# Attention: a unit's inverted sums are turned by their transfer to DRAM, not on TensorE, and the order is planned anew

## The chip, the cores and the metric

The kernel runs on one core of one Trainium2 chip. The metric is the device time of one execution in microseconds; lower is better. The engines are TensorE (PE, with its weight loads shown as PEld), VectorE (DVE), ScalarE (ACT), GpSimd (POOL) and SyncE (SP). SP computes nothing: it issues most transfers, one after the other, and waits in order for what each needs. The transfers themselves run on 16 DMA engines.

## The reference

One layer of a diffusion transformer over 1,024 latent tokens (width 1,024) with 256 context tokens, all in float32. Both attention branches have 8 query heads of width 64 in 2 groups of 4, one key and value head for each group:

- branch 0 (A): keys within 128 tokens of the query, and all 256 context keys; a "sink" logit for each head joins the softmax's sum;
- branch 1 (B): all 1,024 + 256 keys, queries and keys normalised (RMS).

```python
def _sink_softmax(scores, sink):
    sink = sink.astype(jnp.float32)[:, :, None, None]
    m = jnp.maximum(jnp.max(scores, axis=-1, keepdims=True), sink)
    e = jnp.exp(scores - m)
    return e / (jnp.sum(e, axis=-1, keepdims=True) + jnp.exp(sink - m))

def _global_attention(q, k_all, v_all):       # blocks of 128 queries
    ...
        p = jax.nn.softmax(_gqa_scores(q_blk, k_all), axis=-1)
        return _gqa_values(p, v_all)
```

Both branches' outputs go through a matrix each, are weighted by sigmoid gates, merged and projected; then come a residual with layer norm, a feed-forward block with a convolution of width 3 over the tokens, and another layer norm. The change touches only the division by the softmax's sum.

## The kernel before

The kernel has three stages: the projections (to about 325 us of the profiled execution), attention with the branch matrices of branch 0 and part of branch 1 (to about 732 us), and the merge, the projection, the feed-forward block and the norms (to the end).

**Units.** Attention is cut into 32 units, `Unit(br, i, g)`: units 0 to 15 are branch 0, units 16 to 31 branch 1; `i` is the block of 128 queries, `g` the group of four heads. A unit does this:

- POOL splits its queries into a high part that TensorE's fast float32 form keeps and the rest (`qhi`, `qlo`). PE turns them (`qtr`), ACT copies them (`qcp`), and two SP transfers make a second copy with the halves of its partitions swapped (`qdm`, lines 747 and 748, "the `q` swap"). Only then can the unit's scores be computed.
- For each head PE computes scores (`sc`, lines 759 and 760), DVE takes them out of PSUM with their maximum (`pm`), and ACT takes the exponential with its sum (`ex`). The sums of the four heads are the columns of a tile `sm`, 128 partitions (queries) by 4.
- DVE inverts them (`norm`, lines 819 to 821, planned as `nr`).
- PE turns the exponentials block by block (`tr`, line 847) into the `pt` buffers of PSUM. ACT or POOL makes a high part and DVE or POOL the rest, and PE multiplies both with the values (`av`, line 856). This output has the head's width on its partitions and the four heads' queries along its rows.
- ACT copies it out (`avs`), POOL adds its halves (`up`, `ot`, line 861), multiplies them with the inverted sums (`tt`, line 1259), and splits the product for the branch matrix (`oh`, `ol`).

**The inverted sums on their way.** The multiplication `tt` needs them along the row, the same in every partition of a head, while `sm` has the queries on partitions. Before the change, four steps do this:

1. `st` (line 824): PE turns `sm` into 4 rows of 128 in a `pt` buffer of PSUM.
2. `rc` (line 829): ACT copies these into the first partitions of `rb`.
3. `dn` (line 833): SP writes them to a DRAM tile of 4 x 128.
4. `rb` (line 837): after `dn` has landed, SP reads them back twice, each time to 64 partitions with the same two rows in all of them.

```python
def turn(self, tr):
    nc.tensor.transpose(tr[0:4, 0:P], self.sm, ident)
    self.str = tr

def row(self, rb):
    self.rb = rb
    nc.scalar.copy(rb[0:4, 0], self.str[0:4, 0:P])

def rowout(self):
    self.dn = dpool.tile([4, P], F32, tag=f"dn{self.id}", name=f"dn{self.id}")
    nc.sync.dma_start(self.dn, self.rb[0:4, 0])
```

**What sets the order.** In the attention stage no engine's order follows the text. `graph` makes all steps with their dependences, buffers and keys (`KEY`, in units of a unit's number: `st` of unit 3 in branch 0 has the key 3 + 1.27). `plan` then goes through time: on each engine it takes, among the next `LOOK` = 24 steps in the order of keys that could start, the one with the smallest key within `SLACK` of the earliest start. How long a step holds its engine and when its result is there comes from `COST`, for example `dn=(SP, .30, 2.2)`: it holds SP for 0.30 us and has landed 2.2 us after its start. The steps are then issued in the order of their planned starts, and each engine runs them in that order, whatever the true durations are. `FILL` places the groups of the branch matrix among the units of branch 1. Rings of buffers limit how far engines run ahead: 3 `pt` buffers, 2 of `s`, 1 of `av`, 2 of `rb`, 2 each of `q1` and `q2` (the queries and their swapped copy).

Of the kernel before, what the change touches and what calls it, by code (L numbers as in the profile page):

```python
# [13 lines left out]
P = 128  # L14
# [25 lines left out]
PWB = 5  # L40
DAH = 3
SINK = 640
POOLED, FILL, SUMS = ((0,), (1, 6)), (16.988136, 27.931), ('ot1', 'ot1')
LOOK, SLACK = 24, (0, 0, 0, 0, 0)
D3AT = (7, 5), (7, 9), (4, 1), (4, 4), (4, 7), (4, 10), (5, 2)
NXS = 5
RAWB = 3
# [18 lines left out]
PE, ACT, DVE, POOL, SP = range(5)  # L66
# [19 lines left out]
def plan(ops, rings, free, look, slack):  # L86
    todo = [sorted((o for o in ops if o.eng == e), key=lambda o: o.key) for e in range(5)]
    for o in ops:
        for b in o.uses:
            b.left += 1  # L90
    port, done = 0.0, []
    while any(todo):
        best = None
        for e in range(5):
            ready = []
            for o in todo[e][:look]:
                if any(d.end is None for d in o.after):
                    continue
                r = max([free[e]] + [d.end for d in o.after] + [b.free(rings) for b in o.takes])
                if o.port:  # L100
                    r = max(r, port)
                if r < BIG:
                    ready.append((r, o))
            if ready:
                least = min(r for r, _ in ready) + slack[e]
                pick = min((c for c in ready if c[0] <= least), key=lambda c: c[1].key)
                if best is None or pick[0] < best[0]:
                    best = pick
        r, o = best
        todo[o.eng].remove(o)  # L110
        o.start, o.end = r, r + o.lat
        free[o.eng] = r + o.occ
        if o.port:
            port = r + o.occ
        for b in o.takes:
            b.slot = rings[b.ring].index(b.free(rings)) if b.fix is None else b.fix
            rings[b.ring][b.slot] = BIG
        for b in o.uses:
            b.left -= 1
            b.end = max(b.end, o.end)  # L120
            if b.left == 0:
                rings[b.ring][b.slot] = b.end
        done.append(o)
    return sorted(done, key=lambda o: o.start)
# [4 lines left out]
    sc0=(PE, .70, .945), sc1=(PE, .91, 1.16), scx=(PE, .94, 1.19),  # L129
    pm0=(DVE, .80, .97), pm1=(DVE, 1.26, 1.43), pmx=(DVE, .40, .56),  # L130
    ex0=(ACT, .83, .98), ex1=(ACT, 1.14, 1.30), exx=(ACT, .49, .65),
    nr0=(DVE, .18, .28), nr1=(DVE, .34, .44), st=(PE, .11, .36), rc=(ACT, .20, .34), dn=(SP, .30, 2.2),
    rb=(SP, 1.25, 3.1),
    tr=(PE, .436, .685), hi=(ACT, .47, .675), lo=(DVE, .605, .765), cp=(ACT, .47, .675), ph=(POOL, .59, .70),
    pl=(POOL, 1.27, 1.38), avh=(PE, .233, .485), avl=(PE, .233, .485),
# [8 lines left out]
PRING = "pt", "s", "av"  # L144
RINGS = dict(pt=3, s=2, av=1, qs=1, q1=2, q2=2, p=8, hi=4, lo=4, ptr=2, up=1, ot=1, rb=2, wraw=1, wh=1, wl=1)

KEY = {'qh': -0.919337, 'qt': -1.197497, 'sc': -0.139853, 'scs': (0.199825, 0.270357),
           'scx': -3.142963, 'tr': 0.868828, 'tru': (0.216182, 0.070723),
           'av': 1.348883, 'st': 1.265771, 'out': 0.885708, 'exd': 1.273589, 'st1': 1.664154, 'wb': (27.969376, 29.459582),
           'wg': (31.81419, 33.291489, 33.170198, 33.528645), 'ge': -0.046198, 'gr': 4.26668}  # L150
UNITS = 32


def graph(x, key=KEY, pooled=((3,), (2, 6)), fill=None, ot=("ot0", "ot1")):
    ops, last = [], {}
    def op(kind, k, fn, after=(), takes=(), uses=()):
        e, occ, lat = COST[kind]
        o = Op(e, kind, occ, lat, k, fn, after, takes, uses, kind in PORT)
        ops.append(o)
        return o  # L160
# [10 lines left out]
    for hf in (0, 1):  # L171
        b = Buf("pt", 2) if hf == 0 else Buf("av", 0)
# [5 lines left out]
        for c in range(4):  # L178
            r = op("gr", key["gr"] + .6 * (4 * hf + c), lambda hf=hf, c=c: x.gr(hf, c), [e], uses=[tile])
        op("gd", key["gr"] + .6 * (4 * hf + c), lambda hf=hf: x.gd(hf), [r], uses=[tile])  # L180
    units = []
    for u in range(UNITS):
# [10 lines left out]
        if u >= 2:  # L193
            qs, pt = Buf("qs"), Buf("pt")
# [11 lines left out]
        p = {}  # L206
        nar = br == 0 and w == 256
        other = []
        if br:
            s, pc = Buf("s"), Buf("p")  # L210
# [8 lines left out]
        for h in range(4):  # L219
            k = U + key["sc"] + key["scs"][br] * h  # L220
            s = Buf("pt" if nar and h < 2 else "s")
# [27 lines left out]
                sums.append(e)  # L249
        kn = U + (key["st"], key["st1"])[br]  # L250
        n_ = op(f"nr{br}", kn - .05, lambda u=u: x.norm(u), sums)
        pt, rb = Buf("pt"), Buf("rb")
        t = op("st", kn, lambda u=u, p=pt: x.st(u, p), [n_], [pt])
        r = op("rc", kn, lambda u=u, p=pt, b=rb: x.rc(u, p, b), [t], [rb], [pt])
        dn = op("dn", kn, lambda u=u: x.dn(u), [r], uses=[rb])
        rbd = op("rb", kn, lambda u=u: x.rb(u), [dn], uses=[rb])
        rbd.lat = 6.0 if 17 <= u < 30 else 4.2
        av = Buf("av")
        avo, trs = [], []
        for j, n in enumerate(kt):  # L260
            k = U + key["tr"] + j * key["tru"][br]
            ka = U + key["av"] + j * key["tru"][br]
            pt, hi, lo = Buf("pt"), Buf("hi"), Buf("lo")
# [31 lines left out]
        f = op("ol", ko, lambda u=u: x.ol(u), [e], uses=[o_])  # L295
# [5 lines left out]
    for f2 in range(4):  # L301
# [5 lines left out]
        for f in (2 * f2, 2 * f2 + 1):  # L307
            for hf in (0, 1):
                k = f0 + (f1 - f0) * n / 16
                n += 1  # L310
                pt = Buf("pt")
# [10 lines left out]
    for f2 in (0, 1):  # L322
# [5 lines left out]
        for n in (2 * f2, 2 * f2 + 1):  # L328
            pt = Buf("pt")
# [19 lines left out]
def rings():  # L349
    return {n: [0.0] * c for n, c in RINGS.items()}  # L350
# [3 lines left out]
def layer_kernel(  # L354
# [6 lines left out]
    nc = tc.nc  # L361
# [20 lines left out]
    def ctile(shape, dt, name):  # L382
        return const.tile(shape, dt, tag=name, name=name)

    ident = ctile([P, P], F32, "ident")
# [35 lines left out]
    def ht(name, shape=(P, T), dt=F32):  # L421
        hslot[name] = pool, tag = hfree.pop(0)
        return pool.tile(list(shape), dt, tag=tag, name=name, bufs=1)
# [38 lines left out]
    sc, scc = ht("sc"), ht("scc")  # L462

    def spread(dst, src, n):
        row = ht(f"row{n}")
        hput(f"row{n}")
        nc.scalar.dma_start(row, src.partition_broadcast(P))
        nc.scalar.activation(dst, row, AF.Silu)
# [6 lines left out]
    def mod(w, row, bias, o):  # L475
        nc.vector.tensor_tensor_reduce(out=w, in0=w, in1=row, scale=1.0, scalar=bias, op0=ALU.mult, op1=ALU.add,
                                       accum_out=o)
# [6 lines left out]
    st1 = {}  # L484
# [38 lines left out]
    for n in (0, 1):  # L523
        s = slice(n * HALF, (n + 1) * HALF)
# [11 lines left out]
    for k in range(KT):  # L536
# [5 lines left out]
        for t in range(NT):  # L542
            s = slice(t * P, (t + 1) * P)
# [167 lines left out]
    class Unit:  # L711
# [108 lines left out]
                nc.vector.tensor_tensor(out=self.sm, in0=self.sm, in1=self.smc, op=ALU.add)  # L820
            nc.vector.reciprocal(self.sm, self.sm)

        def turn(self, tr):
            nc.tensor.transpose(tr[0:4, 0:P], self.sm, ident)
            self.str = tr

        def row(self, rb):
            self.rb = rb
            nc.scalar.copy(rb[0:4, 0], self.str[0:4, 0:P])  # L829

        def rowout(self):
            self.dn = dpool.tile([4, P], F32, tag=f"dn{self.id}", name=f"dn{self.id}")
            nc.sync.dma_start(self.dn, self.rb[0:4, 0])

        def rowin(self):
            for a in range(2):
                nc.sync.dma_start(self.rb[a * HD:(a + 1) * HD],
                                  self.dn.rearrange("(b a) q -> a b q", a=2)[a].partition_broadcast(HD))
# [49 lines left out]
    units = [Unit(br, i, g) for br in (0, 1) for i in range(NT) for g in range(2)]  # L888
# [80 lines left out]
    turn = [0]  # L969
# [21 lines left out]
    def at(n, fn, *only):  # L991
        if n < len(steps) and (not only or steps[n][0] in only):
            gi, k, a = steps[n]
            fn(*((gi, k) if only else (gi, k, a)))
# [13 lines left out]
    for n, (gi, k, a) in enumerate(steps):  # L1008
# [21 lines left out]
        for t in tiles:  # L1030
            if t < NT:
                s = slice(t * P, (t + 1) * P)
                x = hT[k][0][:, s], hT[k][1][:, s]
            else:
                s = slice((t - NT) * P, (t - NT + 1) * P)
                x = c[0][:, s], c[1][:, s]
# [46 lines left out]
    def small(name):  # L1083
# [3 lines left out]
                 rb=[P, 2, P], wraw=[P, 8, P], wh=[P, 8, P], wl=[P, 8, P])  # L1087
# [42 lines left out]
    class Issue:  # L1130
# [67 lines left out]
        def norm(self, u):  # L1198
            units[u].norm()

        def st(self, u, p):
            units[u].turn(at(p, f"s{units[u].id}"))

        def rc(self, u, p, b):
            units[u].row(at(b, units[u].id))

        def dn(self, u):
            units[u].rowout()

        def rb(self, u):  # L1210
            units[u].rowin()

        def tr(self, u, n, p):
            units[u].ptr(n, at(p, f"{units[u].id}_{n}"))
# [86 lines left out]
    rwb = {}  # L1301
    for o in plan(graph(Issue(), KEY, POOLED, FILL, SUMS)[0], rings(), [0.0, 2.2, 0.0, 0.0, 0.0], LOOK, SLACK):
        if o.fn:
            o.fn()
# [83 lines left out]
    wb = {2: [wq.tile([P, 8, P], R32, tag="w", name=f"{a}wb2", bufs=4) for a in "hl"]}  # L1388
# [661 lines left out]
    s = LN2_S[-1]  # L2050
# [22 lines left out]
    r = LN2_S[1]  # L2073
# [10 lines left out]
    u, ot = [], []  # L2084
# [20 lines left out]
    for t in range(nt):  # L2105
        q = slice(s.start - HALF + t * P, s.start - HALF + (t + 1) * P)
        y = sml(f"yt{t}")
        for k in range(NH):
            h, l = d3[k]
# [122 lines left out]
```

## Time and profile before

| | us |
|---|---|
| median of 3 runs | 1521.83 |
| lowest, highest | 1521.33, 1522.35 |
| the profiled execution | 1522.45 |
| its span, from first to last instruction | 1520.6 |
| mean granted TensorE clock | 0.998 of full |

Busy time in the span: PE 1507.5 us (99%), PEld 1267.1 (83%), DVE 1154.0 (76%), ACT 800.3 (53%), POOL 784.7 (52%).

How to read the rows: a row of a timeline has the start in us from the span's beginning, the duration in us, the engine, the line of the kernel, the operation and its tiles (written<-read). A row of a tile's or line's view has the durations of its instructions in ns (least/median/most) and the first and last start. "PEld" is a weight load, which overlaps the matmul before it. "SPq" is SP's own queue: its duration is that of issuing, not that of the data's way. A matmul's shown duration reaches from its entry into the array to its end, and the next one enters before that, so that work on PE is counted from start to start. In a row of waits, the number after the colon is the time in all, then how many waits, then the longest.

### The profile page before, as it was taken

The page shows a single profiled execution, that of the slowest core. Times are in us where ns is not written, and L with a number is a line of the kernel's source. Part 1 is how long each engine was busy: PE and PEld are TensorE (multiplying, and loading weights), DVE is VectorE, ACT ScalarE, POOL GpSimd, SP SyncE. Part 2 cuts the span into 40 slices and gives each one's busy share as a digit, 9 for nine tenths or more (in the row PEclk, how much of TensorE's full clock was granted, in tenths as well). Part 3 has the DMA queues.
Part 4 walks back from the last instruction along what each step waited for, and adds up shares of the span by engine and source line. Part 5 has one row for each costly group of instructions (what it writes and reads, how often), then busy time and mean ns, then how long its engine had stood idle before and what let it go on. Part 6 is the DMA issues. An engine that isn't in the chain of part 4 may idle for free.

```text
span 1520.6 us, 21967 instructions
## 1 busy us (share of the span) xinstructions
PE 1507.5 (99%) x7640; PEld 1267.1 (83%) x7640; DVE 1154.0 (76%) x1735; ACT 800.3 (53%) x1406; POOL 784.7 (52%) x743
## 2 busy tenths in 40 slices
PE   9999999999999999999999999999999999999997
PEld 7888888889988888888888998888888888888886
DVE  7588847629777777787675888988888888657897
ACT  6422223448987777788233564444444444435533
POOL 0375303428896666585533556666677774021053
PEclk9999999999999999999999999999999999999999
DMA  9767673312447654823460322333344446996723
GB/s 376 257 220 256 219 242 110 94 40 66 119 119 170 170 122 105 175 66 105 154 166 22 108 90 101 111 112 111 111 111 111 111 111 192 368 270 207 253 80 111
DMA packets 112161, 229.73 MB, mean 151 GB/s; under 512 B 13521, under 2 KB 27345, under 8 KB 111954
## 3 DMA queue, kind: packets, MB, share of 16 engines
q1 hardware_dynamic: 97040, 199.72, 40.0%
q0 software_dynamic: 10400, 20.19, 8.6%
q10 hardware_dynamic: 4610, 8.42, 1.5%
q8 instruction: 60, 0.98, 0.3%
q14 instruction: 51, 0.42, 0.1%
HBM read 177.09 MB, written 65.87 MB: 160 GB/s over the span
## 4 chain that ended last, share of the span: by engine, by line
PE 44%; DVE 4%; issue 1%; DMA 1%; ACT 1%; POOL 0%; DVEq 0%; SPq 0%; ACTq 0%
PE p L377 3%; PE p L378 3%; PE p L376 3%; PE c L376 2%; PE a L376 2%; PE d L376 2%; PE a L378 2%; PE d L378 2%; PE c L378 2%; PE d L377 2%; PE c L377 2%; PE a L377 2%; PE y L378 2%; PE y L376 2%; PE y L377 2%; PE u L376 1%
## 5 line engine op out<-in xcount | busy, mean ns | idle before, releaser
L1234 DVE TENSOR_TENSOR lo<-pt,hi 128x512 fp32r<-128x512 f32 x188 | 126.8, 686 | 44.4 <-ACT hi L1228 35.0
L373 DVE TENSOR_TENSOR ld<-rd,hd 128x1024 fp32r<-128x1024 f32 x77 | 97.6, 1284 | 49.1 <-ACT hd L368 47.0
L1228 ACT CAST hi<-pt 128x512 fp32r<-128x512 f32 x188 | 108.4, 582 | 41.8 <-PE pt L847 23.5
L368 ACT CAST hd<-rd 128x1024 fp32r<-128x1024 f32 x77 | 79.5, 1050 | 86.5 <-PE p L378 53.0
L856 PE MATMUL av<-hi,VT 128*128 128x512 f32 x236 | 104.3, 443 | 0.2 <-POOL hi L1223 0.2
L377 PE MATMUL p<-ld,hd 128*128 128x512 f32 x264 | 102.8, 389 | 0.5 <-DVE ld L373 0.5
L376 PE MATMUL p<-hd 128*128 128x512 f32 x264 | 103.2, 391 | 0.0
L378 PE MATMUL p<-hd,ld 128*128 128x512 f32 x264 | 102.8, 389 | 0.0
L376 PE MATMUL g<-hh,whg 128*128 128x512 f32 x256 | 99.9, 390 | 0.0
L377 PE MATMUL g<-hl,whg 128*128 128x512 f32 x256 | 99.6, 389 | 0.0
L378 PE MATMUL g<-hh,wlg 128*128 128x512 f32 x256 | 99.6, 389 | 0.0
L856 PE MATMUL av<-lo,VT 128*128 128x512 f32 x236 | 99.3, 422 | 0.1
L373 POOL TENSOR_TENSOR wlg<-wg,whg 128x512 fp32r<-128x512 f32 x32 | 45.1, 1415 | 101.1 <-ACT whg L368 89.4
L793 DVE TENSOR_SCALAR_CACHE_REDUCE p<-s,cvt,nmc 128x1024 f32<-128x1024 f32 x64 | 85.6, 1339 | 11.0 <-PE s L760 7.1
L847 PEld LDWEIGHTS pt<-ident,p 128*128 128x128 f32 x512 | 63.6, 140 | 17.6 <-ACT rb L829 0.4
L802 ACT ACTIVATE p<-p,nm 128x1024 f32<-128x1024 f32 x64 | 73.9, 1155 | 7.0 <-DVE p L793 6.5
L847 PE MATMUL pt<-ident,p 128*128 128x128 f32 x512 | 76.6, 272 | 0.1
L759 PE MATMUL s<-KL,q 128*128 128x512 f32 (+2 forms) x186 | 72.9, 392 | 0.0
L793 DVE TENSOR_SCALAR_CACHE_REDUCE pa<-s,negsink 128x640 f32<-128x640 f32 (+1 forms) x58 | 49.3, 853 | 29.2 <-PE s L760 28.7
L368 ACT CAST wS<-s 128x512 fp32r<-128x512 f32 x76 | 45.3, 621 | 48.5 <-POOL s L1564 47.7
L760 PE MATMUL s<-KL,q 128*128 128x512 f32 (+2 forms) x186 | 69.5, 374 | 0.0
L368 ACT CAST wA<-ru 128x512 fp32r<-128x512 f32 x57 | 35.5, 623 | 63.0 <-PE d L378 34.8
(438 smaller groups left out, 5044.0 us busy)
## 6 DMA issues: line engine op xcount, KB each, us to landing
wml<-in_wmodT_dram SPq DMA_DIRECT2D x48, 512.0 KB
ru<-in_w_up_dram SPq DMA_DIRECT2D x38, 512.0 KB
rd<-td SPq DMA_DIRECT2D x55, 256.0 KB
rd<-sd SPq DMA_DIRECT2D x44, 256.0 KB
rd<-in_w_dn_dram SPq DMA_DIRECT2D x33, 256.0 KB
wm<-in_wmodT_dram SPq DMA_DIRECT2D x16, 512.0 KB
wg<-in_w_g_dram SPq DMA_DIRECT2D x32, 256.0 KB
q<-q SPq DMA_DIRECT2D x64, 128.0 KB
```

What stands on the lines that cost most here:

```text
L368: cast[:] = [nc.scalar.copy(hi, src).ins]
L373: low[:] = [lo_eng.tensor_tensor(out=lo, in0=src, in1=hi.bitcast(F32), op=ALU.subtract).ins]
L376: nc.tensor.matmul(ps, a[0], b[0], start=start, stop=False, skip_group_check=resumed)
L377: nc.tensor.matmul(ps, a[0], b[1], start=False, stop=False, skip_group_check=resumed)
L378: return nc.tensor.matmul(ps, a[1], b[0], start=False, stop=stop, skip_group_check=resumed).ins
L759: nc.tensor.matmul(o, self.q1[:, hs], ks, start=True, stop=False)
L793: nc.vector.tensor_scalar(out=p if self.br else p[:, self.pad + 1:SINK + 1], in0=self.sv[h], scalar1=self.scale()[:, hs] if self.br else - ...
L802: nc.scalar.activation(o, i, AF.Exp, bias=self.nm[:, hs], scale=-1.0, accum_out=acc)
L847: nc.tensor.transpose(tr[:, h * P:(h + 1) * P], src, ident)
L856: nc.tensor.matmul(self.av, v, self.parts[n][low], start=first, stop=self.left == 0)
L1228: nc.scalar.copy(hi, units[u].parts[n])
L1234: e.tensor_tensor(out=lo, in0=src, in1=hi.bitcast(F32), op=ALU.subtract)
```

## The change

`turn` and `row` are gone, with the steps `st` and `rc` and the `pt` buffer that they held. `rowout` writes `sm` itself to the DRAM tile, with the tile's axes exchanged in the transfer's description: each of the 128 partitions has 4 floats that lie side by side, and they go to 4 addresses 512 bytes apart. `dn` waits for the reciprocal on DVE. The buffer `rb` is taken when the read-back is issued, no longer by ACT's copy. The read-back itself, the multiplication and all other steps are the same. The planner's `dn` holds SP for 0.30 us as before and lands after 4.0 instead of 2.2. Most of the keys, the two `FILL` times and two of the five `SLACK` values (ACT and DVE) are new, and with them the order of the whole attention stage.

```diff
-POOLED, FILL, SUMS = ((0,), (1, 6)), (16.988136, 27.931), ('ot1', 'ot1')
-LOOK, SLACK = 24, (0, 0, 0, 0, 0)
+POOLED, FILL, SUMS = ((0,), (1, 6)), (17.267264, 27.78666), ('ot1', 'ot1')
+LOOK, SLACK = 24, (0, 0.016527, 0.098053, 0, 0)
...
-    nr0=(DVE, .18, .28), nr1=(DVE, .34, .44), st=(PE, .11, .36), rc=(ACT, .20, .34), dn=(SP, .30, 2.2),
+    nr0=(DVE, .18, .28), nr1=(DVE, .34, .44), dn=(SP, .30, 4.0),
...
-KEY = {'qh': -0.919337, 'qt': -1.197497, 'sc': -0.139853, 'scs': (0.199825, 0.270357),
-           'scx': -3.142963, 'tr': 0.868828, 'tru': (0.216182, 0.070723),
-           'av': 1.348883, 'st': 1.265771, 'out': 0.885708, 'exd': 1.273589, 'st1': 1.664154, 'wb': (27.969376, 29.459582),
-           'wg': (31.81419, 33.291489, 33.170198, 33.528645), 'ge': -0.046198, 'gr': 4.26668}
+KEY = {'qh': -2.009729, 'qt': -1.279234, 'sc': -0.167109, 'scs': (0.213269, 0.256195),
+           'scx': -3.695704, 'tr': 0.735325, 'tru': (0.220675, 0.074497),
+           'av': 1.227507, 'st': 1.142197, 'out': 0.987038, 'exd': 1.391503, 'st1': 1.590244, 'wb': (27.681509, 30.223499),
+           'wg': (32.289232, 33.486164, 33.232712, 34.010444), 'ge': 0.606541, 'gr': 4.688437}
...
-        pt, rb = Buf("pt"), Buf("rb")
-        t = op("st", kn, lambda u=u, p=pt: x.st(u, p), [n_], [pt])
-        r = op("rc", kn, lambda u=u, p=pt, b=rb: x.rc(u, p, b), [t], [rb], [pt])
-        dn = op("dn", kn, lambda u=u: x.dn(u), [r], uses=[rb])
-        rbd = op("rb", kn, lambda u=u: x.rb(u), [dn], uses=[rb])
+        rb = Buf("rb")
+        dn = op("dn", kn, lambda u=u: x.dn(u), [n_])
+        rbd = op("rb", kn, lambda u=u, b=rb: x.rb(u, b), [dn], [rb])
...
-        def turn(self, tr):
-            nc.tensor.transpose(tr[0:4, 0:P], self.sm, ident)
-            self.str = tr
-
-        def row(self, rb):
-            self.rb = rb
-            nc.scalar.copy(rb[0:4, 0], self.str[0:4, 0:P])
-
         def rowout(self):
             self.dn = dpool.tile([4, P], F32, tag=f"dn{self.id}", name=f"dn{self.id}")
-            nc.sync.dma_start(self.dn, self.rb[0:4, 0])
-
-        def rowin(self):
+            nc.sync.dma_start(self.dn.rearrange("h q -> q h"), self.sm)
+
+        def rowin(self, rb):
+            self.rb = rb
```

More of the change, by code (lines that the diff above doesn't have):

```diff
@@ L1199, in norm, with rb @@
             units[u].norm()
[L1201 to L1205, printed above, removed]
         def dn(self, u):
             units[u].rowout()
-        def rb(self, u):
-            units[u].rowin()
+        def rb(self, u, b):
+            units[u].rowin(at(b, units[u].id))
         def tr(self, u, n, p):
```

## The prediction

> **What bounds the kernel now.** I looked first at where the changed lines run (the instructions on the tile `sm`: 325.7 to 715.8 us), then at the busy time of each engine over that attention stage, cut into its branch-0 part, its branch-1 part and its end.
>
> ```profile
> core 0: us, PE busy (x) PEld busy (x) DVE busy (x) ACT busy (x) POOL busy (x), PEclk, DMA share, GB/s
> 325.00:461.00 136.00, 135.66 (x925) 122.39 (x924) 104.78 (x230) 114.51 (x264) 113.27 (x165) 1.00 0.35 96
> 461.00:661.00 200.00, 200.00 (x1178) 167.54 (x1177) 147.77 (x306) 148.64 (x323) 123.71 (x154) 1.00 0.61 140
> 661.00:732.00 71.00, 70.88 (x425) 59.41 (x424) 52.11 (x104) 57.37 (x126) 48.51 (x62) 1.00 0.35 95
> ```
>
> TensorE (PE) is busy for 406.5 of 407 us at the full granted clock. ACT, the next, has 114.51 of 136 us in branch 0 and 148.64 of 200 in branch 1. But a busy share can hide short waits, since a matmul's shown duration overlaps the next one's. So the next view is the list of waits of PE and of its weight loads in 325 to 735 us (who waited, for whom; us in total, times, longest):
>
> ```profile
> PE av L856 <- POOL hi L1223: 0.2, 1, 0.2
> PEld av L856 <- POOL lo L1234: 1.0, 3, 0.4
> PEld av L856 <- POOL hi L1223: 0.6, 1, 0.6
> PEld pt L847 <- ACT rb L829: 0.4, 1, 0.4
> ```
>
> These four rows add to 2.2 us. The stage is as long as its PE instructions: taking PE work out shortens it, taking work off any other engine does not.
>
> **The change part by part.**
>
> *The turning on TensorE goes (line 824).* The rows of that group and of the other small steps of a unit, from the views of their tiles and lines (duration in ns: min/median/max):
>
> ```profile
> L821 DVE RECIPROCAL sm<-sm x32: 168/178/179, 325.7 to 715.8; 128x4 f32<-128x4 f32 x32
> L824 PE MATMUL pts<-ident,sm x32: 270/272/276, 336.8 to 717.5; 128*4 128x128 f32 x32
> L829 ACT COPY rb<-pts x32: 238/251/255, 337.7 to 718.3; 4x128 f32<-4x128 f32 x32
> L833 SPq DMA_DIRECT2D dn<-rb x32: 245/246/336, 337.9 to 718.6; - x32
> L885 SPq DMA_DIRECT2D sd<-in_w_dn_dram x6: 611/612/1176, 404.5 to 605.8; - x6
> ```
>
> 32 x 272 ns would be 8.7 us, but that counts the pipeline's depth. What one turning takes out of the PE stream is read from starts in the timeline, once without and once with it:
>
> ```profile
> 419.55 0.29 PE L760 MATMUL s<-KC,q 128*128 128x256 f32 x1
> 419.67 0.60 PE L847 MATMUL pt<-ident,pa 128*128 128x128 f32 x4
> ...
> 421.16 0.28 PE L760 MATMUL s<-KC,q 128*128 128x256 f32 x1
> 421.27 0.27 PE L824 MATMUL pts<-ident,sm 128*4 128x128 f32 x1
> 421.38 0.60 PE L847 MATMUL pt<-ident,pa 128*128 128x128 f32 x4
> ```
>
> From `L760` to `L847` it is 0.12 us without and 0.22 us with the turning; from `L824` to what follows 0.11. I take 0.11: 32 x 0.11 = 3.5 us on the path that sets the end.
>
> *The copy on ScalarE goes (line 829).* 32 x 0.25 = 8.0 us of ACT, with a PSUM buffer of the `pt` ring held from the turning to the copy. ACT is not the bound, so this is worth only what it made PE wait: the one row with `rb L829`, 0.4 us. ACT's 114.51 us in branch 0 is the cover; it was not on the path, so losing it costs nothing.
>
> *The transfer `dn` changes shape and waits for another engine.* Now 4 pieces of 512 B, from 4 partitions; then 512 pieces of 4 B, from 128 partitions. No row has such a transfer. Two costs need bounds.
>
> First, SP's issue. The low end is today's 0.25 us. The nearest row by number of pieces is `L885` (1 MB in 512 pieces of 2 KB), 0.61. I take 0.61: 0.36 us more per unit, on SP alone. The far end is four times that row, 2.4 us, if each of the four columns cost as much; the limit of rival C would fall by the 1.8 between them.
>
> Second, the time from the end of its issue until it has landed, called L below. SP waits that long before the read-back `rb`, and every later SP transfer is behind it. SP's timeline in branch 0 has the spread of today's L:
>
> ```profile
> 414.63 0.24 SPq L833 DMA_DIRECT2D dn<-rb  x1
> 418.97 1.28 SPq L837 DMA_DIRECT2D rb<-dn  x2
> 420.34 0.55 SPq L747 DMA_DIRECT2D q<-q  x1
> 420.94 0.59 SPq L748 DMA_DIRECT2D q<-q  x1
> 422.41 0.25 SPq L833 DMA_DIRECT2D dn<-rb  x1
> 423.61 1.29 SPq L837 DMA_DIRECT2D rb<-dn  x2
> ```
>
> 423.61 - 422.66 = 0.95 us is the quick case, 418.97 - 414.87 = 4.1 us the slow one. For the new shape I take 2.5, between the two: more pieces than the quick case, the same queue as the slow one. The far end is open above; the rival below has its price.
>
> What stands behind SP's wait is the `q` swap of a later unit, without which its scores cannot begin. The slow case above shows what a late one costs. ACT's copy, the PE steps around the first use, and the use of `rb` on POOL:
>
> ```profile
> 418.22 0.59 ACT L743 CAST q<-pt 128x512 fp32r<-128x512 f32 x1 [0.42 <-PE pt L738]
> ...
> 424.26 0.48 PE L856 MATMUL av<-hi,VT 128*128 128x512 f32 x1
> 424.58 0.34 PE L759 MATMUL s<-KL,q 128*128 128x384 f32 x1
> 424.76 0.34 PE L760 MATMUL s<-KL,q 128*128 128x384 f32 x1
> ...
> 422.30 1.53 POOL L861 TENSOR_TENSOR ot<-ptra,up 64x256 f32<-64x256 f32 x2
> 423.91 0.74 POOL L1259 TENSOR_TENSOR ot<-ot,rb 128x256 f32<-128x256 f32 x1
> ```
>
> The swap was ready at 418.81 and went out at 420.34, 1.5 us late behind `rb`; its scores began at 424.58, 0.32 us behind the `av` matmul before them, and no row of PE's waits names a score matmul (`s`). So L = 4.1 costs PE nothing, and at 2.5 I cost the transfer at zero. What hides it is SP's idle time: from 414.63 to 422.41 a unit has 7.78 us, and SP issues 0.24 + 1.28 + 1.19 of it.
>
> *`dn` starts earlier.* It waits for the reciprocal on DVE and no longer for turning and copy: in branch 1 these came late, so `rb` gains room. The multiply on POOL that reads `rb` starts at 423.91, right at the end of the sums (422.30 + 1.53 = 423.83), though `rb` was issued only at 418.97: the row factor was not the late one. An earlier start gains nothing at the end of a unit. On SP, `dn` now passes ahead of whatever was issued between the reciprocal and the copy. What is behind it waits for DVE where it waited for ACT:
>
> ```profile
> SPq L833 <- ACT rb L829: 168.7, 32, 13.0
> SPq L837 <- DMA dn<-rb: 54.1, 29, 5.6
> SPq L747 <- ACT q L743: 47.2, 12, 36.9
> ```
>
> SP spends 168.7 us standing before `dn`; that row disappears, the second grows by 32 x (2.5 - 54.1/32) = 26 us, and SP stays idle enough.
>
> *The new order.* Its keys, two slack values and the time that the planner gives `dn` (2.2 to 4.0) change; which step moves where cannot be read from them. In the order of now PE loses 2.2 us in all, so a better order has at most that to win, and nothing limits what a worse one loses. I take no change beyond the 0.4 above.
>
> **Sum.** Against the profiled execution's 1522.45 us (span 1520.6 and 1.85 around it): -3.5 - 0.4 = -3.9, so 1518.55. That execution is 0.62 above the median of the three runs, 1521.83; for the median I predict 1517.9 us. Ends of this case: all four PE waits go too (-3.5 - 2.2 = -5.7, 1516.1); or the new order adds as much as the largest row of waits, 1.0, and the 0.4 stays (-2.5, 1519.3).
>
> **The rivals.**
>
> *A, nothing comes of it.* PE's 0.11 us a unit turn into idle time because another engine paces the units. For it: POOL has 113.27 of 136 us in branch 0, and the change takes nothing off it. Against: a unit shorter by 0.11 of 7.78 us raises that share from 83 to 84%. Time: 1521.8.
>
> *B, the new order waits for its own reasons.* Place: `av` matmuls, where all waits but one stand now. The planner gives SP 0.30 us for `dn` where I expect 0.61, and its order was fitted to the steps as it costs them. The longest wait of the row with three is 0.4 us; one such wait in each of the 32 units is 12.8 - 3.5 = +9.3, 1531; in half of them +2.9, 1524.7. It decides from 0.11 us per unit on. Against it: the same planner left 2.2 us in 407.
>
> *C, slower: SP is held too long by `dn`.* With the issue at 0.61, a branch-0 unit leaves 7.78 - 0.61 - 1.28 - 1.19 = 4.7 us for L. Each microsecond above that is 16 us over the sixteen units; branch 1, with few units and a long period, stays out of the sum. At L = 6: 16 x 1.3 - 3.5 = +17, 1539. It decides from L = 4.9. For it: even 2 KB in 4 pieces once took 4.1. Against: on the quick path 0.95, and a swap that is issued between `dn` and `rb` gives 1.2 us more.
> At four times the slow case, L = 16.4, the same price is 16 x 11.7 - 3.5 = +184 us, 1706; it gets 0.03 of this rival's chance.
> The Trainium skill (DMA: Bandwidth & Descriptors, Rules for kernel authors) speaks against this change: a last dimension with a step becomes one descriptor per element, and turning data by a plain rearranged transfer is put at 19 times worse than the hardware's own transpose. By it, an estimate, L would be 19 x 0.95 = 18 us and the time some 1731 us; no run here shows such a transfer yet.
>
> **How the numbers follow.** A measurement of this kernel tells about 0.2%, 3.0 us, from no change. The forecast has 0.50 (0.42 of it beyond 3.0 us faster, 0.08 within), A 0.12 (within), B 0.22 (0.20 slower, 0.02 within), C 0.16 (slower, 0.03 at the far price included). That makes faster 0.42, same 0.22, slower 0.36. The forecast's own range is 1516.1 to 1519.3. The 8-in-10 range runs from its lower end, 1516, to B's full price, 1531, and leaves out C and the little above B, under 0.2.
>
> **What would show it.** PE busy still equal to the window's length in the stage, and the stage's last `L821` some 3.5 us earlier than 715.8: the main term. `dn` near 0.6 us in SP's rows, and from its end to `rb` between 1 and 4 us: the transfer's terms. SP's wait before `rb` near 80 us in total. Wrong would be: new rows of PE or PEld waiting, for POOL, DVE or a DMA on `q`, that add to more than 4 us (B, or C when they name the DMA), or `rb` issued over 4.9 us after `dn`.

## The result, and the profile after

The changed kernel takes 1621.04 us (median of 4 runs, 1612.34 to 1621.82) against 1521.58 us before: ratio 1.064, interval 1.062 to 1.066. It is 99 us slower. The forecast was 1517.9 us, 3.9 us faster, and the measured time lies outside the range of 1516 to 1531 us.

The profiled execution has a span of 1618.8 us. First the busy time of each engine in the attention stage. The stretch of 325 to 832.2 us answers to 325 to 732 before: it holds 2,496 of PE's matmuls, and the other one 2,524 with the 32 turnings. The first row is of the changed kernel, the second of the kernel before:

```profile
core 0: us, PE busy (x) PEld busy (x) DVE busy (x) ACT busy (x) POOL busy (x), PEclk, DMA share, GB/s
325.00:832.20 507.20, 429.10 (x2496) 365.57 (x2495) 307.97 (x639) 317.58 (x681) 281.66 (x373) 0.92 0.55 93
325.00:732.00 407.00, 406.54 (x2524) 349.34 (x2523) 304.67 (x639) 320.52 (x711) 285.49 (x377) 1.00 0.47 118
```

The stage is 100 us longer. PE stands for 507.2 - 429.1 = 78.1 us of it. The other 22 us are in its busy time, which rose from 406.5 to 429.1 us although 32 turnings are gone, at a mean granted clock of 0.92. The loss is not all at one place. These are the inversion of unit 15, the last of branch 0, before, and those of units 15 and 31 after, from the timelines of DVE (start, duration, both in us). Unit 31's before started at 715.85, the end of the range in the prediction's row of line 821:

```profile
448.30 0.17 DVE L821 RECIPROCAL sm<-sm 128x4 f32<-128x4 f32 x1
```

```profile
512.77 0.17 DVE L819 RECIPROCAL sm<-sm 128x4 f32<-128x4 f32 x1
...
815.99 0.18 DVE L819 RECIPROCAL sm<-sm 128x4 f32<-128x4 f32 x1
```

Unit 15 is 64.5 us later and unit 31 100.1, so branch 0 lost some 64 us and branch 1 some 36.

What PE waits for, in the changed kernel (waits of matmuls in 325 to 832 us: us in all, times, longest). Before, this list had 0.2 us:

```profile
PE s L758 <- DMA q<-q: 39.8, 6, 12.9
PE av L847 <- POOL hi L1208: 15.5, 3, 8.0
PE sx L758 <- DMA q<-q: 14.2, 3, 10.7
PE av L847 <- POOL lo L1219: 4.8, 6, 1.7
PE pt L758 <- DMA q<-q: 3.4, 2, 3.1
```

57.4 of the 77.7 us in these rows are for the `q` swap. The views of line 823 (the new transfer) and of SP's waits say why the swap is late (landing is counted in us from the start of the issue; the trace has it for 14 of these 32 transfers):

```profile
L823 SPq DMA_DIRECT2D dn<-sm x32: 360/398/587, 326.2 to 816.5; - x32
DMA to landing us min/median/max: 8.5/10.8/13.3
```

```profile
SPq L828 <- DMA dn<-sm: 285.7, 32, 17.7
SPq L823 <- DVE sm L819: 49.3, 14, 27.7
```

The issue is cheap, 0.40 us, but the 2 KB land only after 8.5 to 13.3 us. SP stands before the read-back (line 828) for 285.7 us, where it stood for 54.1. One place of SP's timeline, and the PE row that waited there:

```profile
376.59 0.55 SPq L745 DMA_DIRECT2D q<-q  x1
377.20 0.59 SPq L746 DMA_DIRECT2D q<-q  x1
377.89 0.53 SPq L823 DMA_DIRECT2D dn<-sm  x1
378.51 0.52 SPq L745 DMA_DIRECT2D q<-q  x1
379.08 0.59 SPq L746 DMA_DIRECT2D q<-q  x1
388.47 1.28 SPq L828 DMA_DIRECT2D rb<-dn  x2
```

```profile
382.24 0.66 PE L758 MATMUL s<-KL,q 128*128 128x384 f32 x1 [12.93 <-DMA q<-q]
```

From `dn` at 377.89 to `rb` at 388.47 are 10.6 us, with the two transfers of one swap between. The scores at 382.24 had waited 12.93 us for the swap before it, which had gone out at 376.59 and 377.20. That swap stood behind the read-back of the unit before, which itself had waited for its `dn`.

PE's clock follows that wait. These are the busy times in it, in the 2.8 us behind it and after those:

```profile
372.00:382.00 10.00, 0.00 (x0) 0.00 (x0) 0.00 (x0) 0.00 (x0) 3.39 (x6) 0.50 0.31 66
382.20:385.00 2.80, 2.76 (x10) 2.56 (x11) 0.00 (x0) 0.09 (x1) 0.00 (x0) 0.50 0.00 0
385.20:395.00 9.80, 9.80 (x68) 8.88 (x67) 8.98 (x18) 8.66 (x19) 5.93 (x9) 1.00 0.08 15
```

The granted clock is 0.50 while PE stands and still in the first 2.8 us of work behind the wait. The score matmul of 382.24 takes 0.66 us there, where matmuls of its shape took 0.34 before. So a wait costs more than its own length, and PE's busy time grows.

### The profile page after: what moved, and what is told of

Its sections match the earlier page's. It is cut to its first block, busy times and chain, and to the rows that moved or that the text cites. A ratio compares the mean times of both kernels' runs of the same rounds, so it can differ in the third digit from the quotient of the medians.

```text
span 1618.8 us, 21856 instructions
## 1 busy us (share of the span) xinstructions
PE 1529.6 (94%) x7608; PEld 1283.6 (79%) x7608; DVE 1147.5 (71%) x1735; ACT 796.8 (49%) x1374; POOL 780.0 (48%) x743
## 3 DMA queue, kind: packets, MB, share of 16 engines
q0 software_dynamic: 10400, 20.19, 10.8%
## 4 chain that ended last, share of the span: by engine, by line
PE 82%; DMA 10%; DVE 2%; POOL 2%; issue 2%; ACT 2%; SPq 1%; DVEq 0%; POOLq 0%; ACTq 0%
DMA q<-q 4%; PE av L847 4%; DMA dn<-sm 4%; PE pt L838 4%; PE g L374 4%; PE g L376 4%; PE g L375 4%; PE p L375 3%; PE p L376 3%; PE p L374 3%; PE c L376 2%; PE a L376 2%; PE d L376 2%; PE d L374 2%; PE a L374 2%; PE c L374 2%
## 5 line engine op out<-in xcount | busy, mean ns | idle before, releaser
L1213 ACT CAST hi<-pt 128x512 fp32r<-128x512 f32 x188 | 109.6, 587 | 88.8 <-PE pt L838 78.1
L758 PE MATMUL s<-KL,q 128*128 128x512 f32 (+2 forms) x186 | 72.3, 389 | 39.8 <-DMA q<-q 39.8
L847 PE MATMUL av<-lo,VT 128*128 128x512 f32 x236 | 104.9, 451 | 4.9 <-POOL lo L1219 4.8
L374 PE MATMUL g<-hh,whg 128*128 128x512 f32 x256 | 99.9, 390 | 0.0
L838 PE MATMUL pt<-ident,p 128*128 128x128 f32 x512 | 78.1, 276 | 0.0
L757 PE MATMUL s<-KL,q 128*128 128x512 f32 (+2 forms) x186 | 75.6, 407 | 0.0
L758 PEld LDWEIGHTS s<-KL,q 128*128 128x128 f32 x186 | 36.7, 197 | 47.9 <-issue 22.3
```

The lines of the kernel that those rows point to most:

```text
L374: nc.tensor.matmul(ps, a[0], b[0], start=start, stop=False, skip_group_check=resumed)
L757: nc.tensor.matmul(o, self.q1[:, hs], ks, start=True, stop=False)
L758: nc.tensor.matmul(o, self.q2[:, hs], ks, start=False, stop=stop)
L838: nc.tensor.transpose(tr[:, h * P:(h + 1) * P], src, ident)
L847: nc.tensor.matmul(self.av, v, self.parts[n][low], start=first, stop=self.left == 0)
L1213: nc.scalar.copy(hi, units[u].parts[n])
```

## The experiments

Three theories at the start. W: SP is held until the 512 small writes have landed, the swaps behind it come late and PE waits. O: the new order is what waits. D: the small pieces slow the DMA engines for every transfer. All experiments start from the changed kernel. Those with an interval ran several times, beside the kernel before (1521.43 us there); the others have a single run.

**Fewer pieces: rows16.**

```diff
-            nc.sync.dma_start(self.dn.rearrange("h q -> q h"), self.sm)
+            nc.sync.dma_start(self.dn.rearrange("h q -> (h q)").rearrange("(q h) -> q h", h=4), self.sm)
```

> The changed kernel with its new order, but the transfer writes 128 pieces of 16 bytes (the tile as it lies) in place of 512 pieces of 4 bytes; the read-back then holds the inverted sums in the wrong places, so the division is wrong, and all instructions and bytes are the same in number. Theory W (SP is held until the 512 small writes have landed, the q swaps behind it come late and PE waits): the transfer lands within 1 to 3 us, PE's waits go, and the time is what I predicted for the change, 1517.9, give or take 3 us. Rival O (the new order is what waits): over 1600 us as before. Rival D (the small pieces slow the DMA engines for all transfers): a quarter of the pieces, so a quarter of the 99 us lost, some 1546 us.

Measured: 1519.65 us, ratio 0.9986 (0.9977 to 0.9995), 2.1 us faster than before by the ratio. The view of its transfer, and the largest waits of PE and its weight loads in 325 to 735 us:

```profile
L823 SPq DMA_DIRECT2D dn<-sm x32: 319/326/543, 325.4 to 714.5; - x32
DMA to landing us min/median/max: 1.4/1.9/5.9
```

```profile
PEld av L847 <- POOL lo L1219: 3.0, 5, 1.1
PE av L847 <- POOL lo L1219: 1.4, 3, 0.8
```

With fewer, longer pieces for the same 2 KB, the 99 us are gone. Order, keys and dependences are those of the changed kernel, so O falls. What the transfer does until it has landed is the cause.

**The old order with the new transfer: turned_old.** The keys, fill times, slack and `dn=(SP, .30, 2.2)` of the kernel before are put back.

> The turned transfer with the keys, fill times, slack and planned time of the kernel before (2.2 us for the transfer); only turning and copy are gone. Theory W: at least as slow as the changed kernel, 1600 to 1660 us, since this order expects the transfer still sooner. Rival O: about 1518 us. Rival D: 1600 to 1640 us.

Measured: 1611.40 us in its one run, with SP's wait before the read-back at 289.8 us. The order of before does not help either. Its transfer, the same 512 pieces, landed after 7.4 us in the quickest case and 9.0 in the median.

**No wait for the landing: no_wait.**

```diff
-                                  self.dn.rearrange("(b a) q -> a b q", a=2)[a].partition_broadcast(HD))
+                                  units[max(0, units.index(self) - 2)].dn.rearrange("(b a) q -> a b q", a=2)[a].partition_broadcast(HD))
```

> The changed kernel with all its transfers of 512 pieces, but a unit reads back the DRAM row of the unit two before it, which landed long ago (the division then uses another unit's sums). SP has nothing to wait for between the two transfers. Theory W: 1518 us, give or take 5, with the small transfers still there and still slow to land. Rival O: over 1600 us. Rival D: over 1600 us, since every small piece is still written.

Measured: 1573.16 us, ratio 1.034 (1.032 to 1.036). All three theories missed. SP's wait before the read-back is 18.8 us in all and no longer 285.7, and still 51 us of the loss stay. PE's waits for the swap in 325 to 800 us:

```profile
PE s L758 <- DMA q<-q: 20.6, 3, 9.3
PE sx L758 <- DMA q<-q: 8.8, 2, 6.4
```

One of these waits, with the second transfer of the last swap that had gone out before it:

```profile
397.22 0.59 SPq L746 DMA_DIRECT2D q<-q  x1
```

```profile
406.69 0.41 PE L758 MATMUL s<-KL,q 128*128 128x384 f32 x1 [3.32 <-DMA q<-q]
```

ACT had copied the queries at 396.64, so this swap went out at once, and the scores could begin only 9.5 us later. So there are two mechanisms: SP's standing, and something that the small writes do to other transfers. They are not cleanly apart here, because SP still stands elsewhere: before line 876, for a load of weights, it waits 63.0 us, where it was 31.2 in the changed kernel and 10.6 in rows16. The swap's own landing shows the second mechanism too, in the views of line 745, first of the changed kernel (the trace has 12 of its 32 landings) and then of rows16 (26 of 32):

```profile
L745 SPq DMA_DIRECT2D q<-q x32: 462/548/597, 270.1 to 785.6; - x32
DMA to landing us min/median/max: 2.6/5.9/10.2
```

```profile
L745 SPq DMA_DIRECT2D q<-q x32: 461/501/557, 269.1 to 683.6; - x32
DMA to landing us min/median/max: 2.2/2.3/7.8
```

The DMA engines are also busy for longer with the same bytes. By the rows of the stage their mean busy share was 0.47 of 407 us before and 0.55 of 507.2 us in the changed kernel, 191 and 279 us, for 47.8 and 47.2 MB. In no_wait it is 0.62 of the 455 us from 325 to 780, 282 us, for 104 GB/s x 455 us = 47 MB. In spread, below, it is 0.52 of 407, 212 us. That is what theory D named, though none of its prices came out.

**The small writes on another queue: no_wait_act.** As no_wait, and

```diff
-            nc.sync.dma_start(self.dn.rearrange("h q -> q h"), self.sm)
+            nc.scalar.dma_start(self.dn.rearrange("h q -> q h"), self.sm)
```

> As no_wait (a unit reads back the row of the unit two before it, so SP waits for no landing, and the division uses another unit's sums), and the 512-piece transfer is issued by ACT, on ACT's queue. no_wait still took 1573 us, some 51 above the kernel before. Theory Q (what is issued behind the small writes on the same queue lands only after them, so the q swaps come late even when SP does not wait): the q swaps are on another queue now, PE's waits for them go, and the time is 1519 to 1528 us (ACT's issue of 0.4 us a unit is not on the path). Rival E (the DMA engines themselves are held, whatever the queue): 1560 to 1580 us, with PE still waiting for the q swaps.

Measured: 1577.28 us, ratio 1.037 (1.035 to 1.039), no better than no_wait. PE's waits for the swap in 325 to 800 us:

```profile
PE s L758 <- DMA q<-q: 13.7, 4, 5.4
...
PE sx L758 <- DMA q<-q: 3.9, 1, 3.9
PE pt L758 <- DMA q<-q: 2.9, 1, 2.9
```

20.5 us in place of 29.4 in the list above: less, not gone, so another queue does not free the swaps. A swap and the scores that waited for it:

```profile
393.97 0.59 SPq L746 DMA_DIRECT2D q<-q  x1
```

```profile
404.12 0.66 PE L758 MATMUL s<-KL,q 128*128 128x384 f32 x1 [3.99 <-DMA q<-q]
```

From one to the other are some 10 us, which is rival E's picture. The rest of the time is not separated cleanly, because in this kernel ACT also waits in its own order for the inversion that it now sends off, and PE's waits for POOL's low parts are 13.2 us.

The Trainium skill (DMA: Bandwidth & Descriptors, Queues, rings and completion order) says that a transfer's completion mark lands only after every earlier write of that DMA engine, across its queues. By that rule a swap counts as landed no sooner than the small writes ahead of it on the engines that they share. The changed kernel has such a case: the swap's first transfer at 378.51, behind the small writes of 377.89, lands 10.2 us later, at 388.7, when the small writes have just landed. But the late swaps of no_wait and no_wait_act went out 1.3 and 0.6 us ahead of the next small writes (398.53 and 394.59), and over 6 us behind the ones before (390.69 and 387.46). Even with the longest landing of small writes in any trace, 14.6 us in own_lines, the ones before were down by 405.3 and 402.1, ahead of the scores. So the rule alone does not give these waits, and what keeps the DMA engines busy then is not shown.

**The planner told the truth: late_read.** `dn=(SP, .40, 10.0)`, so that the read-back is planned later and other transfers ahead of it.

> The changed kernel, all its work unchanged and right, with the planner told the truth about its transfer: SP held 0.40 us, landed after 10.0 in place of 4.0, so that it plans the read-back later and puts other SP transfers ahead of it. Theory that SP's standing before the read-back is nearly all of the loss: most of the 99 us comes back, 1525 to 1545 us. Theory that half of it is the DMA engines held by the small writes (no_wait: +51 us): no better than no_wait, 1560 to 1600 us.

Measured: 1581.19 us. SP's wait before the read-back falls to 52.3 us, the swap's share of PE's waits to 7.0, and a new wait takes their place. POOL, then PE, in 325 to 832 us:

```profile
POOL ot L1244 <- DMA rb<-dn: 45.1, 19, 9.9
```

```profile
PE av L847 <- POOL hi L1208: 27.0, 10, 6.4
```

Now the factor itself is late for the multiplication. POOL works in order, so the high parts of later blocks stand behind it and PE waits for those. Three orders were run with these small writes: the changed kernel's, the one of before and this. This one gave back the most, 40 us of the 99, and none hid a landing longer than the 7.8 us of a unit.

**Why it lands so late: rows8, spread, own_lines.** rows8 writes 256 pieces of 8 bytes; spread writes the 512 pieces of 4 bytes to 64 bytes each; own_lines writes 512 pieces in the layout of rows16, by two transfers that take every second head. The code below is spread's; its two DRAM tiles are filled before attention.

```diff
+    spt = [dpool.tile([4, P, 16], F32, tag=f"sp{n}", name=f"sp{n}") for n in (0, 1)]
...
+            sp_ = spt[units.index(self) % 2]
-            nc.sync.dma_start(self.dn.rearrange("h q -> q h"), self.sm)
+            nc.sync.dma_start(sp_.rearrange("h q e -> q h e")[:, :, 0], self.sm)
+            self.dn = sp_.rearrange("h q e -> h (q e)")[:, 0:P]
```

> The changed kernel with 256 pieces of 8 bytes (two heads side by side; the division uses misplaced sums). Theory W with a landing that grows with the number of pieces: the quick case about half of 8.5 us, so 4 to 5 us, at the limit of 4.7 us where SP begins to hold the units, and a time of 1518 to 1545 us. If the landing depends on the total size or on the turned layout and not on the pieces, it stays at 8 us and the time over 1590 us. Rival O: over 1600 us. Rival D: half of the loss, some 1570 us.

> The changed kernel with its 512 pieces of 4 bytes, each now written to its own 64 bytes of DRAM and not side by side with fifteen others (the read-back then brings other values, so the division is wrong; two extra transfers fill the two DRAM tiles in the projection stage). Theory N (the landing is long because there are 512 pieces, each taking about 15 ns to be confirmed): the quick landing stays at 8 us or more and the time at 1600 us or more. Rival L (it is long because sixteen pieces share a line of 64 bytes and must wait for each other): the landing falls under 4 us and the time to 1518 to 1535 us.

> The changed kernel with 512 pieces of 4 bytes that lie in DRAM as the tile lies in SBUF (16 bytes of a query side by side), written by two transfers that each take every second head, so that no two neighbouring pieces can be merged; the read-back then holds misplaced sums. Sixteen pieces share 64 bytes as in the changed kernel, but they come from four neighbouring partitions, not from sixteen. Theory S (any sixteen small writes into one line of 64 bytes wait for each other): the transfer lands after 8 us or more and the time is 1600 us or more. Rival A (it is slow where pieces of many partitions, and so of several DMA engines, meet in a line): landing of 1.5 to 4 us, 1519 to 1530 us.

The landings of the three, each from the view of its line, in this order:

```profile
L823 SPq DMA_DIRECT2D dn<-sm x32: 359/376/805, 326.1 to 721.5; - x32
DMA to landing us min/median/max: 2.9/3.6/11.3
```

```profile
L826 SPq DMA_DIRECT2D sp<-sm x32: 360/374/545, 325.8 to 720.1; - x32
DMA to landing us min/median/max: 1.7/2.7/8.9
```

```profile
L824 SPq DMA_DIRECT2D dn<-sm x64: 550/567/1375, 325.3 to 780.7; - x64
DMA to landing us min/median/max: 3.3/7.7/14.6
```

| kernel | pieces | in 64 bytes of DRAM | quickest landing, us | time, us |
|---|---|---|---|---|
| changed | 512 of 4 B | 16 | 8.5 | 1621.04 |
| own_lines | twice 256 of 4 B | 16 | 3.3 for one transfer | 1584.90 |
| rows8 | 256 of 8 B | 8 | 2.9 | 1526.76 |
| rows16 | 128 of 16 B | 4 | 1.4 | 1519.65 |
| spread | 512 of 4 B | 1 | 1.7 | 1524.21 |

spread decides: the same 512 pieces of 4 bytes, set apart, land in 1.7 us at the quickest and not 8.5, so neither their number nor their size alone is the cause. What costs is many small writes close together. One transfer of own_lines puts 8 pieces into 64 bytes and lands in 3.3 us at the quickest, as rows8 with 8 does in 2.9. Its second transfer then fills the same 64 bytes again; the median of both is 7.7 us, and the time is 1584.90. That lies in neither theory's range. In it the neighbours come from four neighbouring partitions and in the changed kernel from sixteen, and both kernels are slow, which speaks against rival A but does not exclude it. That the writes wait for each other in the DRAM is a reading that fits all five; no run shows where they wait. Nor do the runs say what they share: in spread both the distance between pieces (64 bytes) and the whole stretch (32 KB in place of 2) are larger, and nothing between was tried.

**What the removed PE work is worth: rows16_old, dve_turn, dve_plan, dve_planb.** rows16_old is rows16 in the order of the kernel before. dve_turn keeps TensorE and ScalarE out and the transfer quick: DVE turns blocks of 32 by 32.

```diff
-            nc.vector.reciprocal(self.sm, self.sm)
+            n = units.index(self) % 2
+            nc.vector.reciprocal(smw[n][:, 0:4], self.sm)
+            nc.vector.transpose(smt[n], smw[n])
...
-            nc.sync.dma_start(self.dn.rearrange("h q -> q h"), self.sm)
+            t = smt[units.index(self) % 2]
+            for b in range(4):
+                nc.sync.dma_start(self.dn[:, b * 32:(b + 1) * 32], t[b * 32:b * 32 + 4])
```

`smw` and `smt` are four blocks of 32 columns in a constant tile of ones, which is filled again after attention. dve_plan and dve_planb are the same with the planner's costs taken from dve_turn's trace and two other sets of keys.

> The transfer with 128 pieces of 16 bytes (misplaced sums), in the order of the kernel before: its keys, fill times, slack and planned 2.2 us; turning and copy are gone. Against rows16 (1519.65, new order) this separates the order. If the new order costs nothing: the same within 2 us. If the new order's own waits for POOL ate part of the 3.5 us: 1517 to 1518.5. If the old order suits the removed steps worse: 1521 or more.

> A right kernel: the inverted sums are turned by DVE in blocks of 32 by 32 (one instruction a unit behind the reciprocal), and four transfers of 4 partitions by 128 bytes, 16 pieces in all, write the DRAM tile; no turning on PE, no copy on ACT, planned with 0.18 us more of DVE and 1.0 us of SP, landing after 3.5. Theory W with N: landing 1 to 3 us, no held SP, and the 3.5 us of PE work gone: 1517 to 1520 us, so faster than both kernels. If DVE's extra instruction or SP's four issues hold the units, over 1523 us.

> dve_turn (right; turned by DVE, 16 pieces of 128 bytes) with the planner's costs set to its trace (DVE 0.40 and 0.56 us, SP 1.5 us, landed after 3.2) and the order planned anew with other keys, fill times and slack. dve_turn stood level with the kernel before (ratio 1.000), where 3.5 us of PE work had gone. If the missing 3.5 us are the order's own waits: 1517.5 to 1519.5 us, faster than before. If PE's time does not shorten the stage when another engine is given work: 1521 to 1523 us.

> The same kernel as dve_plan in another order found from the same costs. The two orders apart from each other by less than 1 us: what an order costs can be planned to that. By 2 us or more: the order alone moves this kernel by as much as the removed PE work is worth. Each between 1517.5 and 1522 us.

Measured: rows16_old 1521.39 us, ratio 1.000 (0.999 to 1.001); dve_turn 1521.31 us, 1.000 (0.999 to 1.001); dve_plan 1517.52 us, 0.9975 (0.9966 to 0.9984); dve_planb 1517.54 us, 0.9974 (0.9964 to 0.9985). dve_turn lies between the two ranges that were expected for it. The largest waits of PE and its weight loads of dve_turn, and the whole list of dve_plan, in 325 to 735 us:

```profile
PEld av L853 <- POOL hi L1214: 2.5, 3, 2.1
PE av L853 <- POOL hi L1214: 1.8, 1, 1.8
```

```profile
PEld av L850 <- POOL lo L1222: 1.2, 3, 0.6
PE av L850 <- POOL lo L1222: 0.4, 1, 0.4
PEld av L850 <- POOL hi L1211: 0.2, 1, 0.2
```

The removed work shows in full only where the order leaves PE almost no waits. The rows of PE and PEld are not added up, since one wait can stand in both: the longest waits of dve_turn's two rows end at the same moment, 482.08 us. PE's busy time in 325 to 732 us says how much it stood: 407 - 404.35 = 2.65 us in dve_turn, where nothing was won, and 407 - 406.64 = 0.36 us in dve_plan, where it was 3.8 us (1521.43 x 0.0025; 2.4 to 5.2 by the interval). rows16, with 1.51 us of standing, won 2.1. dve_plan and dve_planb differ by 0.02 us, so this is no single lucky order. Whether the truer costs or the new search for an order did it is not separated. DVE's turning costs 0.21 us a unit and no PE time:

```profile
L820 DVE STREAM_TRANSPOSE onesf<-onesf x32: 210/211/215, 324.9 to 712.4; 128x32 f32<-128x32 f32 x32
```

dve_plan leaves out none of the work and is faster than both kernels.

## Why the prediction was wrong

- **Failed: the landing time L.** The step "For the new shape I take 2.5, between the two" is the one that fell. Measured from the end of the issue, as L is defined, it is 8.1 us at the least and 10.4 in the median (8.5 and 10.8 from its start). Its bounds were rows of today's transfer, 4 pieces of 512 B, and I let them carry over to 512 pieces of 4 B side by side. I thought of number and queue, and of where the pieces go in DRAM not at all; spread shows that, at the same number and size, this decides.
- **Failed with it: the transfer costed at zero.** "L = 4.1 costs PE nothing" was a true reading of the trace before, but the cover ends at 4.7 us, by the prediction's own sum.
- **Rival C was what happened.** Its limit of L = 4.7 us agrees with the runs: rows16, spread and rows8, with median landings of 1.9, 2.7 and 3.6 us, stay within 6 us of the kernel before, and the changed kernel is far above. No run lies close to the limit. Its price, 16 x (L - 4.7) - 3.5, gives 88 us with L = 10.8 - 0.4 = 10.4, against 99 measured. But that is two errors that balance: branch 0 lost some 64 us and not 91, and branch 1, which was left out of the sum, lost 36. The chance of 0.16 for it was too small. The page that spoke against this change (the Trainium skill, DMA: Bandwidth & Descriptors, Rules for kernel authors) was right in its direction. Its factor of 19, which I applied to today's quick landing for an estimate of 18 us, was too much: the quickest landing is 8.5 - 0.4 = 8.1 us against 0.95, a factor of 9.
- **Missing: the second mechanism.** No rival said that other transfers near the small writes land late by themselves. In no_wait and no_wait_act 51 and 56 us of the loss stay although no read-back needs the small writes just ahead of it. Not all of it is the swap's own landing, since SP waits longer for other transfers there. The two do not simply add: late_read took most of SP's wait away, and the read-back's lateness paid for it.
- **Missing: the clock.** 22 of the stage's 100 us are PE's longer busy time, at a granted clock that falls to 0.50 in a long wait and stays there for some microseconds of work.
- **Counted twice, without effect on the forecast: one of PE's waits.** Of the four rows that make 2.2 us, the one of PE for `hi` (0.22 us) and the one of its weight load (0.65) end at the same moment, 453.49 and 453.48. Only the lower end of the range used this sum.
- **Right: SP's issue has the size of a small one.** 0.40 us, below the 0.61 that I took.
- **Right, but not in every order: 3.5 us of PE work.** dve_plan and dve_planb reach 1517.5 us, the forecast's size. rows16_old and dve_turn show rival B on the way: an order that does not fit its steps eats these 3.5 us whole. In dve_turn the longest wait is one of `av` for POOL, where B put them.

## What to carry to other kernels

A transfer that turns a tile by its addresses is not priced by its bytes or its pieces: look at how many small writes lie close together in DRAM, and keep them in longer runs or apart. Such writes cost twice here, at the queue that waits for their landing and at other transfers near them; another order gave back 40 of the 99 us and another queue nothing. Where an engine is full to 99.9%, work taken off it shows in full only after the order is planned anew around what replaced it.

## What was unexpected of the hardware

- 512 writes of 4 bytes side by side in 2 KB of DRAM land after 8.5 us at the least (7.4 in turned_old), and the same 512 writes 64 bytes apart after 1.7 us.
- A swap of the queries that goes out near such writes lands after 5.9 us in the median of 12 landings, where it is 2.3 in rows16; issuing the writes on ACT's queue did not free it. The DMA engines are busy for some 90 us more in the stage, for the same bytes.
- The granted clock of TensorE fell with its waiting: 0.92 in the stage of the changed kernel, where PE stood for 78.1 us. In 325 to 732 us of rows8, where it stood for 4.1, it was 0.99, and in rows16, with 1.5, 1.00. Within one long wait it was 0.50 before PE had work again, so the wait came first and the lower clock with it; how long a wait must be for that was not tried.
